# A hybrid diffusion trunk on one core: the two layers' tails put into a written order, the last parts' squares added by TensorE

## The chip, the cores and the metric

The kernel runs as one program on one core of a Trainium2 chip. A core has five engines with instruction streams of their own: TensorE (PE, with its weight loads PEld), VectorE (DVE), ScalarE (ACT), GpSimd (POOL) and SyncE (SP), which here issues the DMA transfers. [...] The metric is device time in microseconds, the median over the executions of a kernel.

## The reference

Two layers run over 1024 latent tokens and 256 context tokens, each of 1024 channels, in float32. What matters here stands at the end of a layer and at the start of the next:

```python
def rmsnorm(t, g):
    y = tf * lax.rsqrt(jnp.mean(tf * tf, axis=-1, keepdims=True) + EPS) * g
def modulate(t, shift, scale):
    return t * (1 + scale) + shift
for l in range(DEPTH):
    ax = modulate(rmsnorm(h, norm1_g[l]), mx[0], mx[1])      # and ac from hc, the context
    yx, yc = mixing_layer(ax @ w_in[l], ac @ w_in[l], ...)
    h = h + mx[2] * (yx @ w_out[l])
    h = h + mx[5] * conv_ffn(modulate(rmsnorm(h, norm2_g[l]), mx[3], mx[4]), w_up[l], ..., w_down[l])
    # the context hc likewise, in layer 0 alone
return rmsnorm(h, final_g)
```

So behind the last product with w_down, layer 0 normalises and modulates h and hc for layer 1, and layer 1 normalises h for the output. A token's mean of squares runs over all its 1024 channels, so no row of a token can be normalised before the last product for that token.

## The kernel before

Activations lie with channels on the 128 partitions and tokens along the free axis: h is eight tiles (k or o = 0 to 7) of 128 x 1024, the context hc eight of 128 x 256. Tokens are worked off in parts: part 0 and 1 are 512 latent tokens each, part 2 the 256 context tokens, and parts 3 and 4 are the two halves of part 1 (256 tokens each). A product in float32 is made of three passes over split operands (high times high, low times high, high times low; L1332 to L1334 in the tail).

The down projection has 22 blocks of 128 hidden channels. Twenty of them run in a loop of five chunks, the main loop (products at L939, each result added to h by VectorE in acc_h, L1244). That stretch stands inside `manual_schedule()`: what is written there keeps the written order on each engine, and a planner with a cost model places all other instructions between. The region is opened by `order.enter_context(tc.manual_schedule())` (L814) and closed by `order.close()` (L1310), right behind the loop.

Behind L1310 comes the tail, placed by the planner. Four operands (two blocks, two parts) are loaded and split by `pair` (copy to a high half L831 on ScalarE, low half L832 on VectorE). The last two blocks are multiplied by `down1(w, part, o)`, once for each part and each output tile o: six matmuls, then acc_h, then `sums[part].add` (L217): ScalarE squares the row (L219, L223), and VectorE or GpSimd adds it to an accumulator (L224). In layer 0 the parts are 0, 1, 2, in layer 1 they are 0, 3, 4.

`stats` (L226) sums the accumulator over partitions with TensorE (tile nps, L230), scales it on VectorE (L232) and takes the power -1/2 on GpSimd (L233). `spread` (L235) turns that into a row on all partitions: VectorE scales the identity by it (dg, L241), TensorE multiplies by ones (npb, L242).

In layer 0, `pipelined` writes: products of a part, its stats, the normalisation of the part before, its spread. The normalisation is `modulated` (L245): for each k one VectorE instruction (nt, L253), then ScalarE makes the high half and VectorE the low half (L260, L261); for k = 1, 4, 7 ScalarE adds the shift (L256) and casts (L257), and GpSimd makes the low half (L258). Rows of parts 0 and 1 are also stored to `h_dram` (L1368).

In layer 1 all three parts' products and sums come first; the scales of parts 0 and 3 are copied to SBUF by ScalarE (L1388), and `final` multiplies each row by gain and scale on VectorE (L1373) and stores it (L1374), part by part.

Scratch tiles (squares, normalised rows, scaled identities, accumulators, copies of scales) share one tag, "nt", with five buffers. PSUM has two banks for tag "g", two for "a", and two double ones for "bc".

Behind layer 0's tail layer 1 starts with products of the first two tiles of w_in (`feed`, L194 to L196), which fill the two "g" banks; ScalarE copies them out (L269, L299). Weights are brought in by `prefetch`, with `load_weights` (copy L179, L180 or L185, low half L181, L182 or L186).

## Time and profile before

| what | value |
|---|---|
| median of three runs | 3044.99 us (3044.64 to 3050.8) |
| profiled execution, its own time | 3046.27 us |
| span of its instructions | 3044.5 us |
| busy: TensorE / VectorE / ScalarE / GpSimd | 92% / 70% / 41% / 45% |
| mean granted TensorE clock | 0.956 |
| layer 0's tail: first product of the last two blocks | 1662.3 us |
| layer 1's tail: last product | 3012.5 us |

The profile gives the instructions of one execution with start, duration, source line and tiles, and infers from semaphores what ended an engine's idle time. Times count from the first instruction. A row of the timeline reads: start, duration, engine, line, operation, output tile <- input tiles, shapes, count, and in brackets idle time before it and what ended it. Neighbouring equal instructions are merged into one row with a count. A row by line gives minimum, median and maximum duration in ns. SPq stands for SyncE's issues of DMA transfers.

### The profile page before, as it was taken

To read this page: it belongs to the slowest core of one execution; us is meant where nothing else is said; L and a number is where in the kernel's file an instruction comes from. 1 tells how busy PE (TensorE), PEld (TensorE's weight loads), DVE (VectorE), ACT (ScalarE), POOL (GpSimd) and SP (SyncE) were. 2 spreads that over 40 slices of the span, in tenths; PEclk is the share of its full clock that TensorE was granted. 3 is DMA by queue.
4 is the path that set the end of the run, shared out by engine and by line. 5 is a ranking of instruction groups with operands and counts; after the bars stand their busy time and mean duration, and the time that the engine had idled before them with its cause. 6 is when DMAs were issued, how large, how long until landed. Compare 5 with 4: busy or idle time off the path is not lost. (4 is left out here: it accounts for less than half of the span.)

```text
span 3044.5 us, 40171 instructions
## 1 busy us (share of the span) xinstructions
PE 2786.5 (92%) x14430; PEld 2335.4 (77%) x14430; DVE 2141.4 (70%) x3484; ACT 1247.2 (41%) x2404; POOL 1357.0 (45%) x894
## 2 busy tenths in 40 slices
PE   6789989989989999998999799989988899998996
PEld 4678877878768888887888688877777688886775
DVE  7887745562777777788877654546557777877996
ACT  4345542232444344444333455542223444444332
POOL 4334343323334455544555244444243455554553
PEclk8899998989999999999999899999899999999998
DMA  6343322032133434346334112131251233336441
GB/s 219 89 113 113 96 87 77 31 141 70 56 104 127 144 127 144 130 142 204 117 125 123 51 46 67 46 103 59 77 180 56 90 118 121 118 114 205 135 145 63
DMA packets 167738, 332.54 MB, mean 109 GB/s; under 512 B 49650, under 2 KB 62834, under 8 KB 167282
## 3 DMA queue, kind: packets, MB, share of 16 engines
q1 hardware_dynamic: 167252, 328.81, 32.9%
q8 instruction: 114, 1.87, 0.2%
q10 hardware_dynamic: 288, 1.18, 0.1%
q14 instruction: 84, 0.69, 0.1%
HBM read 255.72 MB, written 74.19 MB: 108 GB/s over the span
## 5 line engine op out<-in xcount | busy, mean ns | idle before, releaser
L939 PE MATMUL ua<-ph,wu 128*128 128x512 f32 x1408 | 449.9, 401 | 31.4 <-DVE ub L1039 13.4
L165 POOL TENSOR_TENSOR wu<-urb,wu 128x512 fp32r<-128x512 f32 x160 | 244.4, 1528 | 323.8 <-ACT wu L164 323.8
L194 PE MATMUL gps<-xh,wh 128*128 128x512 f32 (+1 forms) x968 | 361.2, 374 | 15.6 <-ACT vt L269 7.0
L165 POOL TENSOR_TENSOR wu<-ura,wu 128x512 fp32r<-128x512 f32 x192 | 305.6, 1593 | 155.2 <-ACT wu L164 155.2
L195 PE MATMUL gps<-xh,wl 128*128 128x512 f32 (+1 forms) x968 | 356.1, 368 | 0.5 <-DVE wl L181 0.5
L196 PE MATMUL gps<-xl,wh 128*128 128x512 f32 (+1 forms) x968 | 355.9, 368 | 0.0
L939 PE MATMUL ubc<-ph,wu 128*128 128x512 f32 x1056 | 332.6, 396 | 15.1 <-DVE ubc L1036 6.5
L939 PEld LDWEIGHTS ua<-ph,wu 128*128 128x128 f32 x1408 | 263.9, 192 | 94.5 <-ACT ut L1033 17.3
L426 POOL TENSOR_SCALAR P<-P,rs 128x640 f32<-128x640 f32 (+2 forms) x108 | 215.6, 2008 | 237.2 <-DVE rs L421 130.3
L165 POOL TENSOR_TENSOR wu<-S,wu 128x512 fp32r<-128x512 f32 x128 | 180.7, 1414 | 248.3 <-ACT wu L164 247.0
L939 PE MATMUL ua<-pl,wu 128*128 128x512 f32 x704 | 280.1, 398 | 0.1
L164 ACT CAST wu<-S 128x512 fp32r<-128x512 f32 x128 | 79.4, 621 | 413.0 <-DVE S L162 404.8
L939 PEld LDWEIGHTS ubc<-ph,wu 128*128 128x128 f32 x1056 | 198.9, 191 | 60.9 <-issue 7.9
L186 POOL TENSOR_TENSOR wl<-wraw,wh 128x1024 fp32r<-128x1024 f32 x54 | 134.4, 2491 | 212.6 <-ACT wh L185 200.1
L194 PEld LDWEIGHTS gps<-xh,wh 128*128 128x128 f32 x968 | 186.9, 193 | 45.3 <-ACT vt L269 7.3
L939 PE MATMUL da<-ph,wu 128*128 128x512 f32 x640 | 202.8, 398 | 12.1 <-ACT wu L164 11.4
L939 PE MATMUL ubc<-pl,wu 128*128 128x512 f32 x528 | 208.3, 395 | 0.0
L195 PEld LDWEIGHTS gps<-xh,wl 128*128 128x128 f32 x968 | 186.6, 193 | 26.6 <-issue 1.0
L196 PEld LDWEIGHTS gps<-xl,wh 128*128 128x128 f32 x968 | 186.2, 192 | 26.1 <-issue 0.5
L164 ACT CAST wu<-ura 128x512 fp32r<-128x512 f32 x192 | 118.9, 622 | 129.3 <-DVE ura L162 72.8
L164 ACT CAST wu<-urb 128x512 fp32r<-128x512 f32 x160 | 99.4, 622 | 168.5 <-DVE urb L162 141.4
L939 PE MATMUL dbc<-ph,wu 128*128 128x512 f32 x480 | 150.7, 395 | 10.8 <-DVE c L1099 10.8
(296 smaller groups left out, 6858.9 us busy)
## 6 DMA issues: line engine op xcount, KB each, us to landing
gs<-g_dram SPq DMA_DIRECT2D x148, 256.0 KB, 2.8
wm<-in_w_mod_dram SPq DMA_DIRECT2D x56, 512.0 KB, 3.6
wmp<-in_w_mod_dram SPq DMA_DIRECT2D x112, 256.0 KB, 2.7
wraw<-in_w_in_dram SPq DMA_DIRECT2D x46, 512.0 KB, 3.6
ura<-in_w_up_dram SPq DMA_DIRECT2D x44, 512.0 KB, 4.2
urb<-in_w_up_dram SPq DMA_DIRECT2D x44, 512.0 KB, 5.2
g_dram<-gt SPq DMA_DIRECT2D x60, 256.0 KB, 3.1
g_dram<-c SPq DMA_DIRECT2D x44, 256.0 KB, 2.0
```

The costliest lines, as they stand in the source:

```text
L164: nc.scalar.copy(w[:, 0], b[name])
L165: nc.gpsimd.tensor_tensor(w[:, 1], b[name], w[:, 0].bitcast(F32), op=ALU.subtract)
L186: nc.gpsimd.tensor_tensor(wl.rearrange(flat), raw.rearrange(flat), wh.rearrange(flat).bitcast(F32), op=ALU.subtract)
L194: nc.tensor.matmul(ps[:, :n], wh[:, k], xh, start=k == 0, stop=False)
L195: nc.tensor.matmul(ps[:, :n], wl[:, k], xh, start=False, stop=False)
L196: nc.tensor.matmul(ps[:, :n], wh[:, k], xl, start=False, stop=k == KT - 1)
L426: nc.gpsimd.tensor_scalar(Pb[r][:, :w], Pb[r][:, :w], rs[:, r:r + 1], None, op0=ALU.mult)
L939: nc.tensor.matmul(ps, lt, rt, start=start and j == 0 and q == 0, stop=j == len(x) - 1 and q == 2, skip_group_check=True)
```

## The change

`order.close()` moves from behind the main loop to the end of the layer, so that the whole tail stands in written order. What is written there:

- `down1` only multiplies; `head(part, between)` runs it for the eight o and, behind each column's update and square, calls the functions listed for that o.
- Layer 0: products of part 0; products of part 1 with stats and spread of part 0 and its rows 0 to 3; products of part 2 with rows 4 to 6 of part 0 and the stats of part 1; row 7; the next weights (`prefetch`); spread and rows of part 1; stats, spread and rows of part 2. A row is one VectorE instruction, ScalarE's high half, and VectorE's low half (`settle`, one row behind) for every k; GpSimd makes no low halves here. The squares of part 0 are added by VectorE, those of parts 1 and 2 by GpSimd.
- Layer 1: products of part 0 (squares added by VectorE), of part 3 and of part 4. For parts 3 and 4 `add_pe` has no accumulator: TensorE sums each square over partitions straight into one PSUM tile, one column behind (`held`). Rows of part 0 go between the products of part 4; the others follow. For k = 1, 4, 7 of parts 0 and 3, ScalarE multiplies by the gain and GpSimd by the scale (from an SBUF copy made by `spread_copy`); all other rows are VectorE's, with the scale read from PSUM.

```diff
--- before.py
+++ after.py
@@ -213,6 +213,20 @@
             self.pool = pool
             self.part = part
             self.first = True
+            self.ps = None
+
+        def add_pe(self, h, psp, stop):
+            m = self.n // 128
+            if self.first:
+                self.ps = psp.tile([128, 4], F32, tag="bc" if psp is not psg else "g", name="nps")
+            sq = self.pool.tile([128, self.n], F32, tag="nt", name="sq", bufs=NT)
+            nc.scalar.activation(sq, h, AF.Square)
+            first, self.first = self.first, False
+
+            def held():
+                for j in range(m):
+                    nc.tensor.matmul(self.ps[:, j:j + 1], sq[:, j * 128:(j + 1) * 128], ones[:, 0:1], start=first and j == 0, stop=stop, skip_group_check=True)
+            return held
 
         def add(self, h, eng=None):
             if self.first:
@@ -225,8 +239,8 @@
 
         def stats(self, psp, ta):
             m = self.n // 128
-            ps = psp.tile([128, 4], F32, tag=ta, name="nps")
-            for j in range(m):
+            ps = self.ps or psp.tile([128, 4], F32, tag=ta, name="nps")
+            for j in range(m if self.ps is None else 0):
                 nc.tensor.matmul(ps[:, j:j + 1], self.acc[:, j * 128:(j + 1) * 128], ones[:, 0:1], start=True, stop=True)
             self.r = r = self.pool.tile([128, 4], F32, tag="rs", name="rs")
             nc.vector.tensor_scalar(r[:, :m], ps[:, :m], 1.0 / D, EPS, op0=ALU.mult, op1=ALU.add)
@@ -765,7 +779,7 @@
             return hs[0][k][:, o:o + n]
 
         def new_sums(parts):
-            return {part: Sums(part, npl, npl.tile([128, PARTS[part][1]], F32, tag="nt", name="acc", bufs=NT)) for part in parts}
+            return {part: Sums(part, npl, npl.tile([128, PARTS[part][1]], F32, tag="nt", name="acc", bufs=NT) if part < 3 else None) for part in parts}
 
         for k in range(KT):
             hsrc(k, h[k], None if last else hc[k])
@@ -1307,7 +1321,6 @@
                     ust.close()
                     wx = fp.enter_context(tc.tile_pool(name=f"wx{l}", bufs=1, side="right", reuse_waits="tile"))
         put_all()
-        order.close()
         xpool[0] = wx
         p = NF // 2 - 1
         gl_ = {}
@@ -1317,12 +1330,9 @@
             if not last:
                 gl_[i, 2] = gcs[NF - 2 + i]
 
-        def down1(w, part, o):
+        def down1(w, part, o, tag):
             o0, pn = PARTS[part]
-            if o % 2:
-                ps = psf.tile([128, 512], F32, tag="a", name="dps")
-            else:
-                ps = psg.tile([128, 512], F32, tag="g", name="dps")
+            ps = (psg if tag == "g" else psf).tile([128, 512], F32, tag=tag, name="dps")
             for i in range(2):
                 c0 = i * 512 + (o % 4) * 128
                 wh, wl = [t.rearrange("p a b -> p (a b)")[:, c0:c0 + 128] for t in w]
@@ -1332,8 +1342,7 @@
                 nc.tensor.matmul(ps[:, :pn], wh, gh, start=i == 0, stop=False)
                 nc.tensor.matmul(ps[:, :pn], wl, gh, start=False, stop=False)
                 nc.tensor.matmul(ps[:, :pn], wh, gl, start=False, stop=i == 1)
-            acc_h(o, part, ps)
-            sums[part].add(hv(o, part), nc.gpsimd if last and o % 2 else nc.vector)
+            return ps
 
         ws = [weights(), weights()]
         rawpool[0] = None
@@ -1345,50 +1354,93 @@
                 affine(1, 0, cd)
         Xn = [[None] * 3 for _ in range(KT)]
 
-        def pipelined(parts, head, tail):
-            prev = None
-            for part in parts:
-                head(part)
-                sums[part].stats(psf, "bc")
-                if prev is not None:
-                    tail(*prev)
-                prev = (part, sums[part].spread(psf, "bc"))
-            tail(*prev)
-
-        def down_head(part):
+        def head(part, between):
+            held = None
             for o in range(KT):
-                down1(ws[o // 4], part, o)
-
-        def down_tail(part, pb):
+                ps = down1(ws[o // 4], part, o, "a" if o % 2 or part == 4 else "g")
+                if held is not None:
+                    held()
+                acc_h(o, part, ps)
+                held = sums[part].add_pe(hv(o, part), psf if part == 3 else psg, o == KT - 1) if part > 2 else sums[part].add(hv(o, part), nc.vector if part == 0 else None)
+                for fn in between.get(o, ()):
+                    fn()
+            if held is not None:
+                held()
+
+        def modulate(part, ks):
+            n = PARTS[part][1]
+            cd = 1 if part == 2 else 0
+            A, B = aff[1][cd][:, 0:8], mod[1][cd][:, 0:8]
+
+            def go():
+                for k in ks:
+                    t = npl.tile([128, n], F32, tag="nt", name="nt", bufs=NT)
+                    nc.vector.scalar_tensor_tensor(t, hv(k, part), A[:, k:k + 1], pbs[part][:, :n], op0=ALU.mult, op1=ALU.mult)
+                    xh, xl = xtile(part)
+                    nc.scalar.activation(xh, t, AF.Identity, bias=B[:, k:k + 1])
+                    late.append((xl, t, B[:, k:k + 1], xh))
+                    if len(late) > 1:
+                        settle()
+                    Xn[k][part] = xh, xl
+                    if part < 2:
+                        o0 = PARTS[part][0]
+                        nc.sync.dma_start(h_dram[:, k, o0:o0 + n], hv(k, part))
+            return go
+
+        late = []
+
+        def settle():
+            xl, t, b, xh = late.pop(0)
+            nc.vector.scalar_tensor_tensor(xl, t, b, xh.bitcast(F32), op0=ALU.add, op1=ALU.subtract)
+
+        def final(part, ks):
             o0, n = PARTS[part]
-            res = modulated(1, 0, part, [hv(k, part) for k in range(KT)], pb, npl)
-            for k in range(KT):
-                Xn[k][part] = res[k]
-                if part < 2:
-                    nc.sync.dma_start(h_dram[:, k, o0:o0 + n], hv(k, part))
-
-        def final(part, pb):
-            o0, n = PARTS[part]
-            for k in range(KT):
-                nc.vector.scalar_tensor_tensor(hv(k, part), hv(k, part), fg[:, k:k + 1], pb[:, :n], op0=ALU.mult, op1=ALU.mult)
-                nc.sync.dma_start(out[k * 128:(k + 1) * 128, o0:o0 + n], hv(k, part))
-
+
+            def go():
+                for k in ks:
+                    v = hv(k, part)
+                    if part < 4 and k % 3 == 1:
+                        nc.scalar.mul(v, v, fg[:, k:k + 1])
+                        nc.gpsimd.tensor_tensor(v, v, copies[part], op=ALU.mult)
+                    else:
+                        nc.vector.scalar_tensor_tensor(v, v, fg[:, k:k + 1], pbs[part][:, :n], op0=ALU.mult, op1=ALU.mult)
+                    nc.sync.dma_start(out[k * 128:(k + 1) * 128, o0:o0 + n], v)
+            return go
+
+        copies = {}
+
+        def spread_copy(part, pool, tag):
+            spread(part, pool, tag)
+            n = PARTS[part][1]
+            copies[part] = npl.tile([128, n], F32, tag="nt", name="pbs", bufs=NT)
+            nc.scalar.copy(copies[part], pbs[part][:, :n])
+
+        st = lambda part: lambda: sums[part].stats(psf, "bc")
+        head(0, {})
         if last:
-            pbs = {p: npl.tile([128, PARTS[p][1]], F32, tag="nt", name="pbs", bufs=NT) for p in tail_parts[:-1]}
-            done = []
-            for part in tail_parts:
-                o0, n = PARTS[part]
-                down_head(part)
-                sums[part].stats(psf, "bc")
-                if part == tail_parts[-1]:
-                    for p in done:
-                        final(p, pbs[p])
-                    final(part, sums[part].spread(psf, "bc"))
-                else:
-                    nc.scalar.copy(pbs[part], sums[part].spread(psf, "bc")[:, :n])
-                    done.append(part)
+            head(3, {2: (st(0),), 6: (lambda: spread_copy(0, psf, "bc"),)})
+            head(4, {1: (st(3), final(0, (0, 1))), 4: (final(0, (2,)),), 5: (lambda: spread_copy(3, psg, "g"),), 6: (final(0, (3, 4)),)})
+            sums[4].stats(psf, "bc")
+            final(0, (5, 6, 7))()
+            final(3, (0, 1))()
+            spread(4, psf, "a")
+            final(3, range(2, KT))()
+            final(4, range(KT))()
         else:
-            pipelined(tail_parts, down_head, down_tail)
+            sp = lambda part: lambda: spread(part, psf, "bc")
+            head(1, {2: (st(0),), 4: (sp(0), modulate(0, (0,))), 5: (modulate(0, (1,)),), 6: (modulate(0, (2,)),), 7: (modulate(0, (3,)),)})
+            head(2, {2: (modulate(0, (4,)),), 3: (st(1),), 4: (modulate(0, (5,)),), 6: (modulate(0, (6,)),)})
+            modulate(0, (7,))()
+            settle()
+            prefetch()
+            sp(1)()
+            modulate(1, range(KT))()
+            settle()
+            st(2)()
+            sp(2)()
+            modulate(2, range(KT))()
+            settle()
+        order.close()
         fp.close()
         return Xn
 
```

## The prediction

> **What bounds the kernel now.** I read first the times of each engine by stretch (columns: stretch, its length, busy time and instructions of TensorE, its weight loads, VectorE, ScalarE, GpSimd, then granted clock, DMA share, GB/s). The kernel as a whole is TensorE's, 92% busy; the two ends of layers, which the change touches, are not:
>
> ```profile
> 1710.70:1726.80 16.10, 1.99 (x9) 1.45 (x8) 14.52 (x30) 12.49 (x24) 7.63 (x7) 0.65 0.00 1
> ...
> 2991.40:3012.80 21.40, 21.40 (x148) 19.71 (x146) 14.98 (x31) 5.46 (x11) 6.22 (x6) 1.00 0.00 1
> 3012.80:3044.50 31.70, 4.44 (x17) 3.71 (x16) 16.21 (x37) 5.30 (x15) 7.24 (x10) 0.55 0.36 132
> ```
>
> Behind the last product of layer 1 (3012.8) 31.7 us are left in which TensorE does 4.4 us. The chain of waits says what they are, and the list of waits agrees:
>
> ```profile
> 3014.64 3.39 DVE g L1373 x5
> ...
> 3018.89 0.73 POOL acc L224
> 3019.65 0.44 DVE acc L224
> ...
> 3035.43 0.74 POOLq L1657
> 3036.64 1.21 PE npb L242 x4
> ...
> 3038.74 2.35 DVE g L1373 x6
> ```
>
> ```profile
> PE nps L230 <- POOL acc L224: 17.6, 2, 9.5
> ```
>
> The reader is to see a serial chain: final rows of part 0, seven additions of squares of part 3 handed to and fro between GpSimd and VectorE, its scale, its rows, then all of it once more for part 4. TensorE waits 17.6 us for the two sums. Five "nt" buffers hold three sums and two copies of scales in this stretch, so a square gets a buffer late and the additions cannot run ahead.
>
> At the end of layer 0 it is VectorE and what follows it, by the timeline:
>
> ```profile
> 1725.46 0.72 POOL L258 TENSOR_TENSOR xl<-nt,xh 128x256 fp32r<-128x256 f32 x1 [0.92 <-ACT xh L257]
> ...
> 1726.22 0.59 ACT L269 COPY vt<-gps 128x512 f32<-128x512 f32 x1 [0.83 <-POOL xl L258]
> ...
> 1726.86 0.79 PE L194 MATMUL gps<-xh,wh 128*128 128x512 f32 x1 [7.03 <-ACT vt L269]
> ```
>
> Layer 1's products of part 0 already stand in both "g" banks; the copy that empties the first waits for the last normalised row (ends 1726.18). That end is what layer 1 starts from, so layer 0's gain is the shift of 1726.18.
>
> **The change part by part.**
>
> *Start of both tails.* The region of written order now runs on through the tail. The four operands of the last pair of column blocks (VectorE, L832) were pulled forward by the planner; written out, they stand behind the last update of the loop.
>
> ```profile
> 1662.28 0.40 PE L1332 MATMUL dps<-ph,wh 128*128 128x512 f32 x1
> 1662.48 0.48 DVE L1244 SCALAR_TENSOR_TENSOR hd<-dc,mod,hd 128x256 f32<-128x256 f32 x1
> ...
> 1663.44 0.39 PE L1334 MATMUL dps<-pl,wh 128*128 128x512 f32 x1
> 1663.65 2.40 POOL L186 TENSOR_TENSOR wl<-wraw,wh 128x1024 fp32r<-128x1024 f32 x1 [4.49 <-DMA cb<-in_rpbU_dram]
> ```
>
> ```profile
> L832 DVE TENSOR_TENSOR pl<-gs,ph x4: 681/688/694, 1640.7 to 1646.0; 128x512 fp32r<-128x512 f32 x4
> ```
>
> ```profile
> L832 DVE TENSOR_TENSOR pl<-gs,ph x4: 678/1060/1540, 2971.9 to 2979.0; 128x512 fp32r<-128x512 f32 x4
> ```
>
> The first column's last product needs the third of them: 1662.96 + 3 x 0.69 = 1665.0 in place of 1663.44, +1.6 us in layer 0. The next layer's weight subtraction (2.40 us on GpSimd) now falls onto them, and the second L832 row shows what that does: 1.54 us in place of 0.69. Bounds 0 and 2.4 us; I take 1.9, since the subtraction starts before the third.
>
> *Layer 0, parts 0 to 2.* Removed from VectorE: additions of parts 1 and 2 (to GpSimd). Added: all the low halves that GpSimd did for every third row. Moved: normalisation of part 0 into the products of parts 1 and 2. Rows that price it:
>
> ```profile
> 1674.92 0.75 DVE L1244 SCALAR_TENSOR_TENSOR g<-dps,mod,g 128x512 f32<-128x512 f32 x1
> ...
> 1676.32 0.75 DVE L1244 SCALAR_TENSOR_TENSOR g<-dps,mod,g 128x512 f32<-128x512 f32 x1
> ```
>
> ```profile
> 1682.87 1.01 POOL L233 TENSOR_TENSOR rs<-rs,nhalf 128x4 f32<-128x4 f32 x1 [16.82 <-DVE rs L232]
> ```
>
> ```profile
> 1683.91 0.87 DVE L241 TENSOR_SCALAR dg<-ident,rs 128x128 f32<-128x128 f32 x4 [1.12 <-POOL rs L233]
> ```
>
> ```profile
> 1697.48 2.71 DVE L253 SCALAR_TENSOR_TENSOR nt<-g,aff,npb 128x512 f32<-128x512 f32 x4
> ...
> 1715.57 1.41 DVE L261 SCALAR_TENSOR_TENSOR xl<-nt,mod,xh 128x512 fp32r<-128x512 f32 x2
> ...
> 1719.94 1.66 DVE L253 SCALAR_TENSOR_TENSOR nt<-hd,aff,npb 128x256 f32<-128x256 f32 x4
> ```
>
> A column of products takes 1.40 us; a row of 512 needs 0.66 + 0.67 = 1.33 us of VectorE (pitches of L253 and L261), a row of 256 about 0.79, an update 0.66 or 0.40. I count from part 1's first product, 1674.92 - 1.47 = 1673.45 before, 1675.05 with the 1.6. Part 0's scale is asked for at column 2, but its power stands on GpSimd behind the additions of columns 1 and 2 (1.30 us each), so it is ready at about 8; column 4's products end at 7.8, the four VectorE scalings (0.87) and TensorE's spreading end at 10.1, and TensorE waits for them. Then update, row, low half alternate with columns 5 to 7: VectorE is done at 17.4. Through part 2: eight updates 3.2, three rows 4.0, scale 0.1, last row and two low halves 2.0: 26.6. Behind it the next layer's weight half 0.7, spreading of part 1 1.5, eight rows 10.6 and the last low half 0.4: 39.8. Part 2's scale now stands alone in the written order (0.1, power 0.7, scalings 0.5, spreading 1.2, with hand-overs 2.7): 42.5. Eight rows of 256 at 0.79 and a last 0.4: 49.2. End 1724.2, 2.0 us earlier than 1726.18; with the 1.9 above, 0.1.
>
> What speaks against even this is the pairing of VectorE with GpSimd:
>
> ```profile
> 2996.97 1.30 POOL L224 TENSOR_TENSOR acc<-acc,sq 128x512 f32<-128x512 f32 x1 [8.45 <-ACT sq L223]
> ```
>
> ```profile
> L261 DVE SCALAR_TENSOR_TENSOR xl<-nt,mod,xh x15: 472/742/1774, 1695.8 to 1724.7; 128x512 fp32r<-128x512 f32 x10, 128x256 fp32r<-128x256 f32 x5
> ```
>
> The low halves, 0.74 us as a rule, took up to 1.77. In the new order each part 1 or part 2 column sends a square to GpSimd's addition just when VectorE reaches a low half. Seven low halves lie there, three against 1.30 us additions and four against the 0.7 us ones: at worst 3 x 1.1 + 4 x 0.6 = 5.7, at best nothing. By times of arrival they are within 0.1 us of each other, so I take half, 2.8. Layer 0: -2.0 + 1.9 + 2.8 = **+2.7 us**, between -2.0 and +6.1.
> [...]
>
> *Layer 1.* Fourteen products of this tail stood inside the loop, in front of the loop's last products:
>
> ```profile
> L1332 PE MATMUL dps<-ph,wh x6: 389/392/397, 2976.0 to 2988.7; 128*128 128x512 f32 x6
> ...
> L1333 PE MATMUL dps<-ph,wl x4: 392/394/397, 2976.3 to 2982.5; 128*128 128x512 f32 x4
> ...
> L1334 PE MATMUL dps<-pl,wh x4: 390/392/396, 2977.0 to 2982.7; 128*128 128x512 f32 x4
> ```
>
> ```profile
> 2991.39 0.39 PE L939 MATMUL da<-pl,wu 128*128 128x512 f32 x1
> ```
>
> ```profile
> 3005.36 0.48 DVE L1244 SCALAR_TENSOR_TENSOR g<-dps,mod,g 128x256 f32<-128x256 f32 x1 [0.22 <-PE dps L1334]
> 3006.07 0.48 DVE L1244 SCALAR_TENSOR_TENSOR g<-dps,mod,g 128x256 f32<-128x256 f32 x1 [0.23 <-PE dps L1334]
> ```
>
> ```profile
> 3007.30 0.95 PE L230 MATMUL nps<-ones,acc 128*128 128x1 f32 x8
> 3008.12 0.36 PE L1332 MATMUL dps<-ph,wh 128*128 128x256 f32 x1
> ...
> 3010.34 1.06 PE L242 MATMUL npb<-dg,ones 128*128 128x128 f32 x8
> ```
>
> ```profile
> 3018.06 0.42 ACT L223 ACTIVATE sq<-g 128x256 f32<-128x256 f32 x1 [4.11 <-DVE g L1373]
> ```
>
> At 1.40 / 6 = 0.23 us each they are 3.2 us. TensorE was fully busy there, so I let the loop end 3.2 earlier (bound: not at all, if they filled stalls): free at 2988.4. Part 0: 8 x 1.38 = 11.0, plus 1.85 for the operands: 3001.25. Part 3: eight columns of 0.71 us, eight sums of squares (four of the eight L230 instructions, 0.45, and 0.05 of change-over: 0.5), sum and spreading of part 0 (0.9 each: eight L230 in 0.82, eight L242 likewise, and change-over), and a last square with nothing in front (0.6): 5.7 + 4.0 + 2.4 = 12.1, to 3013.3. Part 4: 5.7 + 4.0 + spreading 0.5 + 0.6 = 10.8, to 3024.1. A square is ready 1.1 us after its column (update 0.48, square 0.42, hand-overs); the next column and the sum ahead of it cover 0.71 + 0.5 = 1.21, so it costs nothing as long as ScalarE and VectorE are free; if that 0.1 us is gone, each microsecond of lateness counts sixteen times.
>
> Removed: the adding chains behind 3012.8. What remains behind 3024.1 are 19 output rows, bounded by SP's issues:
>
> ```profile
> 3038.37 0.81 SPq L1374 DMA_DIRECT2D out_dram<-g  x2
> ```
>
> ```profile
> 3041.78 0.41 SPq L1374 DMA_DIRECT2D out_dram<-g  x1
> ```
>
> The last eight issues took 3.41 / 7 = 0.49 us apiece while VectorE made a row each 0.39 (2.35 / 6), so SP sets the pace; the span ended 2.3 us behind the last. From the last sum: first issue at +1.0, the third row waits for GpSimd behind its power (+2.4), the rest at 0.49: last issue ends at +10.9, end +13.2, at 3037.3. Layer 1: **-7.2 us**, between -4.0 (the 3.2 us were stalls) and -9.8 (VectorE's rows alone set the end: 10.6 behind the last sum).
>
> *Sum.* +2.7 - 7.2 = -4.5. The profiled execution took 3046.27 us (span 3044.5 and 1.8 around it), so 3041.8 for one like it; it lies 1.3 above the median of 3044.99, so I forecast **3040.5 us**. Its own range is 3036 to 3045.
>
> **The rivals.**
> *Faster.* Additions and low halves miss each other, the weight subtraction comes late enough, and output rows leave as fast as VectorE makes them: -2.0 - 9.8 = -11.8, 3033.2 us. For it: updates read PSUM and never showed a stretched time (0.75 in every row). Against: the L261 row, and 0.49 us for SP.
> *The sums do not shorten the tail.* ScalarE has row products and copies of its own among the squares; if these put each square 0.5 us past its cover, 16 x 0.5 = 8.0 eats the gain of layer 1: 2.7 + 0.8 = +3.5, 3048.5 us. Against it: ScalarE was busy 5.46 of 21.4 us in these products.
> *Slower.* The planner may no longer bring layer 1's first products into the longer written region. Then their 48 (11.0 us at 0.23) come behind the end of layer 0's tail in place of inside it: -4.5 + 11.0 = +6.5, 3051.5 us. It decides once more than about 20 of the 48 (4.5 us) start behind that end. Against it: the fourteen products above came from outside the old region and ran inside it.
>
> **How the numbers follow.** Forecast 0.48, faster 0.30, sums too late 0.10, slower 0.12. A measurement of this kernel can tell about 0.2%, 6.1 us, from no change: faster means under 3038.9, slower over 3051.1. Under 3038.9 lie nearly all of the faster case and a quarter of the forecast's own range: 0.41. Over 3051.1 lies about two thirds of the slower case and a little of the one before: 0.09. The rest, 0.50, is the same. The range 3032 to 3049.5 takes in the faster and the late-sum case and leaves most of the slower one out.
>
> **What would show it.** The L832 operands of both tails behind the last loop update, with TensorE idle about 2 us. Layer 0: the last low half at about 1729, L261 rows over 1.2 us while GpSimd adds. Layer 1: the 16 pairs of sums between columns of 0.71, TensorE busy until about 3024, last issue 0.49 us behind the one before. I am wrong if layer 0's end comes before 1724, if SP is not the last to finish, or if layer 1's first products start only behind the tail.

## The result

The changed kernel takes 3071.22 us (median of 4 executions, 3063.3 to 3075.48), the kernel before 3044.85 (3044.64 to 3050.8) beside it: a ratio of 1.0068, 95% interval 1.0052 to 1.0084 (the ratios here and below are those on record; they are not quotients of the two medians, which here would give 1.0087). It is slower, by more than a measurement of this kernel can confuse with no change, and it lies outside the forecast range (3032 to 3049.5, with 3040.5 forecast).

The profiled execution took 3063.3 us (span 3061.5), the shortest of the four and the one with the highest mean granted clock (0.955; the others 0.950 to 0.954). Since executions lie some 12 us apart, the traces are compared by stretches inside one execution, from one TensorE instruction to another that both kernels have: **A** runs from the 455th product of the group dc to the 1676th of the group gps (layer 0's tail and the first products of the mixing), **B** from the 856th product of the group da to the end of the span (end of the last loop and layer 1's tail). A grew from 120.2 to 129.0 us, B from 99.6 to 113.9. What lies between them took 1173.8 and 1172.2. So both tails lost, 8.8 and 14.3 us, where +2.7 and -7.2 had been forecast.

### The profile page after: what moved, and what is told of

The parts are those of the page before. It is cut to its first block, busy times and chain, and to the rows that moved or that the text cites. A ratio compares the mean times of both kernels' runs of the same rounds, so it can differ in the third digit from the quotient of the medians.

```text
span 3061.5 us, 40260 instructions
## 1 busy us (share of the span) xinstructions
PE 2805.3 (92%) x14486; PEld 2350.8 (77%) x14486; DVE 2134.2 (70%) x3471; ACT 1248.7 (41%) x2401; POOL 1359.0 (44%) x893
## 5 line engine op out<-in xcount | busy, mean ns | idle before, releaser
L953 PE MATMUL ubc<-ph,wu 128*128 128x512 f32 x1056 | 333.2, 397 | 14.7 <-ACT wu L164 6.3
L164 ACT CAST wu<-S 128x512 fp32r<-128x512 f32 x128 | 79.5, 621 | 418.6 <-DVE S L162 394.5
```

The source lines that it names most:

```text
L164: nc.scalar.copy(w[:, 0], b[name])
L953: nc.tensor.matmul(ps, lt, rt, start=start and j == 0 and q == 0, stop=j == len(x) - 1 and q == 2, skip_group_check=True)
```

## The profile after

In layer 1, stretch by stretch (columns: stretch, length, busy time and instructions of TensorE, its weight loads, VectorE, ScalarE, GpSimd, granted clock, DMA share, GB/s):

```profile
2991.00:3003.90 12.90, 11.69 (x51) 8.89 (x50) 9.18 (x14) 3.16 (x5) 0.00 (x0) 1.00 0.00 0
3003.90:3011.40 7.50, 1.85 (x13) 1.44 (x11) 5.07 (x9) 2.35 (x5) 0.00 (x0) 0.83 0.00 0
...
3012.20:3046.30 34.10, 33.31 (x155) 33.05 (x155) 9.65 (x24) 7.12 (x17) 2.97 (x3) 0.50 0.06 24
3046.30:3049.70 3.40, 1.56 (x13) 1.39 (x12) 1.60 (x5) 2.70 (x6) 2.07 (x3) 0.99 0.40 154
```

Before, TensorE was done at 3012.8 and waited for chains of additions. Now it issues almost without a pause for 34.1 us (33.31 busy), at half its clock. Two things come ahead of that: part 0's products are over at 3003.9, and then TensorE does 1.85 us of work in 7.5. VectorE's timeline shows why:

```profile
2995.82 0.75 DVE L1258 SCALAR_TENSOR_TENSOR g<-dps,mod,g 128x512 f32<-128x512 f32 x1 [0.65 <-PE dps L1344]
2997.27 0.69 DVE L238 TENSOR_TENSOR acc<-acc,sq 128x512 f32<-128x512 f32 x1 [0.70 <-ACT sq L237]
2997.88 0.75 DVE L1258 SCALAR_TENSOR_TENSOR g<-dps,mod,g 128x512 f32<-128x512 f32 x1
2999.33 0.69 DVE L238 TENSOR_TENSOR acc<-acc,sq 128x512 f32<-128x512 f32 x1 [0.70 <-ACT sq L237]
2999.93 0.75 DVE L1258 SCALAR_TENSOR_TENSOR g<-dps,mod,g 128x512 f32<-128x512 f32 x1
...
3009.76 0.69 DVE L238 TENSOR_TENSOR acc<-acc,sq 128x512 f32<-128x512 f32 x1 [0.76 <-ACT sq L237]
```

Update, wait 0.70 us for ScalarE's square of the row just updated, addition, next update: a column takes 2.05 us of VectorE (2997.88 to 2999.93) where its products take 1.40. The next update could have run in the wait, but the written order puts it behind the addition. Eight columns later TensorE stands and waits for the square of part 3's first column, whose update came last in that line:

```profile
3011.41 1.01 PE L228 MATMUL nps<-ones,sq 128*128 128x1 f32 x4 [5.59 <-ACT sq L223]
...
3017.55 0.85 PE L228 MATMUL nps<-ones,sq 128*128 128x1 f32 x4
3019.68 0.85 PE L228 MATMUL nps<-ones,sq 128*128 128x1 f32 x4
```

Behind the stall of 5.59 us, a column of part 3 (six products of 256 columns and four one-column matmuls) takes 2.13 us (3017.55 to 3019.68), at the clock of 0.50.

Layer 0 has the same VectorE line, with GpSimd's weight subtractions falling on it:

```profile
1661.02 0.74 DVE L1258 SCALAR_TENSOR_TENSOR g<-dps,mod,g 128x512 f32<-128x512 f32 x1
...
1663.79 2.62 DVE L238 TENSOR_TENSOR acc<-acc,sq 128x512 f32<-128x512 f32 x1 [0.70 <-ACT sq L237]
...
1667.78 0.69 DVE L238 TENSOR_TENSOR acc<-acc,sq 128x512 f32<-128x512 f32 x1 [0.70 <-ACT sq L237]
...
1669.83 1.99 DVE L238 TENSOR_TENSOR acc<-acc,sq 128x512 f32<-128x512 f32 x1 [0.70 <-ACT sq L237]
...
1680.12 2.06 DVE L1258 SCALAR_TENSOR_TENSOR g<-dps,mod,g 128x512 f32<-128x512 f32 x3
...
1732.13 0.49 DVE L1394 SCALAR_TENSOR_TENSOR xl<-nt,mod,xh 128x256 fp32r<-128x256 f32 x1 [0.18 <-ACT xh L1380]
```

```profile
1663.48 2.39 POOL L186 TENSOR_TENSOR wl<-wraw,wh 128x1024 fp32r<-128x1024 f32 x1
...
1668.87 2.40 POOL L186 TENSOR_TENSOR wl<-wraw,wh 128x1024 fp32r<-128x1024 f32 x1
```

This execution ran 4.4 us ahead of before's when it came to the tail; the last low half's end, 1732.6, is 1737.0 by before's time, against 1726.18.

## The experiments

The table gives A and B of each profiled execution and the median of all executions of that kernel. The changed kernel was measured beside four executions of the kernel before (median 3044.85), the other kernels on three chips beside 10 to 31 further ones, which ran from 3044 to 3060 us (medians 3050.5 to 3052.1). So a difference from the kernel before is taken from the executions beside it, and A and B tell more than a few us of the median. They scatter too: A is 118.8 to 120.2 in the seven kernels with the planner's layer 0, and 129.0, 129.0 and 132.0 in the three with the changed kernel's (the last with 27.3 us of A at half clock, the other two with 17.1).

| kernel | A | B | median, us | ratio to before, 95% |
|---|---|---|---|---|
| before | 120.2 | 99.6 | 3044.85 | |
| changed | 129.0 | 113.9 | 3071.22 | 1.0068 (1.0052 to 1.0084) |
| additions one column late | 125.2 | 97.2 | 3063.31 | 1.0043 (1.0026 to 1.0060) |
| the stall filled with matmuls | 129.0 | 101.4 | 3062.9 | 1.0040 (1.0023 to 1.0056) |
| written order in layer 0 only | 132.0 | 101.3 | 3063.96 | 1.0049 (1.0034 to 1.0065) |
| written order in layer 1 only | 119.7 | 115.8 | 3064.17 | 1.0038 (1.0021 to 1.0056) |
| layer 1 only, additions late | 119.5 | 109.3 | 3049.13 | 1.0000 (0.9987 to 1.0013) |
| the same, no sums on TensorE | 120.2 | 93.5 | 3044.08 | 0.9975 (0.9964 to 0.9987) |
| both layers, late, operands early | 123.3 | 109.5 | 3060.93 | 1.0034 (1.0017 to 1.0050) |
| layer 1 only, late in turn, operands early | 120.1 | 106.0 | 3054.57 | 1.0014 (1.0001 to 1.0026) |
| the same, no sums on TensorE | 120.2 | 92.8 | 3042.8 | 0.9972 (0.9960 to 0.9985) |
| sums kept, products repeated | 118.8 | 100.0 | 3050.49 | 1.0003 (0.9990 to 1.0016) |
| both layers, a weight split put off | 125.8 | 103.9 | 3059.13 | 1.0028 (1.0012 to 1.0043) |
| both layers mended | 125.0 | 93.5 | 3048.57 | 0.9992 (0.9982 to 1.0002) |

### First theory: the VectorE line stalls TensorE, and the stall costs the clock

**Additions one column late.** In part 0 of both layers, a column's square is added behind the next column's update:

```
+ if held is not None: held()      # the addition of the column before
+ held = sums[0].add_late(hv(o, 0), nc.vector)   # square now, addition later
```

> Edit: in both layers VectorE adds part 0's square one column late, behind the update of the next column; nothing else. Theory A (VectorE's line update-square-add makes a column 2.05 us instead of 1.40; TensorE then stands still 5.6 us before the first sum of squares; behind that standstill its clock stays at half through parts 3 and 4): part 0's columns go to about 1.4 us, the standstill in layer 1 falls under 1 us, the clock stays at 1.0 until the last sum, a column of parts 3 and 4 takes 1.2 us in place of 2.13. Layer 0's tail about 5 us shorter, layer 1's about 5 + 15 = 20 us: some 25 us under the changed kernel, near 3040. Rival B (the one-column sums of squares throttle TensorE by themselves, standstill or not): the columns of parts 3 and 4 still take 2.13 us, only 5 us per layer are won, about 10 us under the changed kernel.

**The stall filled.** The changed kernel, with 24 matmuls that compute nothing of use put into layer 1's stall (extra work):

```
+ if part == 3 and o == 1:
+     busy(24)
```

> Edit: 24 unused matmuls of 128x512 (about 0.23 us each, 5.5 us) stand on TensorE in layer 1 behind part 3's second column, where it stood still for 5.6 us; all else as in the changed kernel. Theory A (the standstill brings the clock down, and the light columns cannot bring it back): the clock stays at 1.0, columns of parts 3 and 4 take 1.2 us, 16 x 0.9 = 14 us under the changed kernel although there is more work. Rival B (the sums throttle by themselves): no change within 2 us.

In both executions profiled the half clock is gone from layer 1's tail. The windows of the kernel with late additions (first its stall, now 1.78 us), and two of its columns:

```profile
3017.50:3020.20 2.70, 0.92 (x9) 0.71 (x7) 2.35 (x5) 1.12 (x3) 0.00 (x0) 1.00 0.00 0
3020.20:3030.40 10.20, 9.86 (x80) 9.44 (x80) 3.69 (x11) 2.99 (x7) 1.01 (x1) 1.00 0.01 2
```

```profile
3024.75 0.61 PE L228 MATMUL nps<-ones,sq 128*128 128x1 f32 x4
...
3026.01 0.50 PE L228 MATMUL nps<-ones,sq 128*128 128x1 f32 x4
```

The same columns now take 1.25 to 1.26 us (3024.75 to 3026.01) at a clock of 1.00, and B is 97.2, under before's. With the stall filled B is 101.4, 12.5 less than in the changed kernel for more work:

```profile
3024.50:3034.60 10.10, 9.76 (x80) 9.25 (x79) 3.40 (x12) 3.21 (x8) 1.01 (x1) 1.00 0.01 2
```

So the tail can run at the full clock, and one-column matmuls do not bring it down by themselves (1.00 was granted from 3020.2 to 3043.6 with late additions, from 3024.5 to 3048.1 with the stall filled). But the medians came down by 8 us only, or by 15 if each is taken over the kernel before beside it (26.4, then 11.2 and 10.8), and not by the 25 that had been expected of the first kernel. The next two kernels say where the rest is.

**One layer at a time.** The written order in one layer, the planner's order of the kernel before in the other:

> Edit: the written order in layer 0's tail alone; layer 1's tail as in the kernel before. By the two traces layer 0's tail lost 9.8 us, so 9 to 11 us over the kernel before, near 3054. If the planner gives it back further on, under 5 us.

> Edit: the written order in layer 1's tail alone; layer 0's tail as in the kernel before. By the two traces layer 1's tail lost 14 us (17 behind the loop, less 3 for the fourteen products that no longer stand in the loop): near 3059, with the clock at half from the first sum of squares on. If the half clock is a matter of the longer way before it, it does not come and the time is near 3042.

The losses add: A is long where layer 0 is written (132.0), B where layer 1 is (115.8), and each kernel is 12 us over the one before beside it (3052.11) by the median. Layer 1 alone has executions at 3054.8 and 3054.85 and four others at 3061.8 to 3068.6: the gap is about what the half clock costs. So an execution seems to fall into the half clock or not. Only one execution of each kernel has records of its stretches, but the mean granted clock over the span is on record for every one: 0.955 and 0.956 in the two short ones, 0.950 to 0.952 in the four others. Thirty us at half clock make 0.005 of it, so the fall fits, though the mean does not say where it lies. By the same number the late additions did less than their trace says: 0.957 in the execution profiled, the shortest, and 0.951 to 0.955 in the other three. With the stall filled all five have 0.956 to 0.959.

### Second theory: sparse columns, and chance

The next four kernels were to find the best version of layer 1, and three of them upset the theory.

**Layer 1 only, additions late.**

> Layer 0 as in the kernel before; layer 1 in the written order, with the addition of a square in part 0 put one column later. Stretch A is from the 455th product of the group dc to the 1676th product of the group gps on TensorE (layer 0's tail and the start of the mixing; 120.2 us before, 129.0 in the changed kernel), stretch B from the 856th product of the group da to the end (layer 1's tail; 99.6 before, 113.9 changed, 97.2 where both layers had the late addition). If the two tails are independent: A about 120, B about 97, and the time 2 to 3 us under the kernel before. If the late addition's gain in layer 1 was the luck of one execution: B scatters between 97 and 114 from one execution to another, and the median lies 3 to 10 us above the kernel before.

**The same without sums on TensorE.** The squares of parts 3 and 4 go back into accumulators, in turn on VectorE and GpSimd, still in the written order:

```
- held = sums[part].add_pe(hv(o, part), ...)
+ held = sums[part].add_late(hv(o, part), nc.gpsimd if part > 2 and o % 2 else nc.vector)
```

> As the run with layer 1 alone and the late addition, but the squares of the last two parts are added into accumulators again, in turn by VectorE and GpSimd, one column late, instead of by one-column matmuls. My theory (the sums on TensorE are harmless at the full clock: 1.25 us a column against 0.71 without them, covered by VectorE and ScalarE): columns of the last parts 0.75 to 1.2 us, set by VectorE and GpSimd; stretch B 94 to 99, within 3 us of the run with the sums on TensorE. Rival (the sums cost what they add to TensorE, 16 times 0.5 us): B about 8 us shorter, near 89. Third: GpSimd's slower addition sets the pace or the lighter TensorE loses its clock, B over 100.

**Operands early, both layers.** The last four operands (L846) are read and split between the loop's last updates; sums on TensorE kept:

```
+ if early and ch == NCH - 1 and half == 1 and i >= len(names) - 4 and i < len(names) - 2:
+     lead(i - len(names) + 4)     # load, then ScalarE's half; VectorE's half follows an update
```

> The changed kernel with the late addition in part 0 of both layers, and with the four operands of the last chunk read and split two to four weight groups earlier, between the loop's last updates, in both layers. If the operands behind the last update lie on the path as forecast (2.49 us on VectorE): stretch B 96 (97.2 with the late addition alone, minus 1.0 to 1.2, since TensorE's first column of 1.4 us then takes their place), stretch A 123 to 124 (125.2 alone). If VectorE's total work is the bound of layer 0's tail, A falls by the whole 2.5 us to 122.7. If something else is late there (TensorE waits for the spread rows): A stays at 125.

**Layer 1 only, operands early, part 0's additions late and in turn on VectorE and GpSimd.**

> Layer 0 as in the kernel before; layer 1 in the written order with the late addition, the additions of part 0 in turn on VectorE and GpSimd, and the operands split early. VectorE then has 1.09 us of work per column of 1.40, so that TensorE doesn't wait at the first sum (1.78 us with all additions on VectorE): stretch B 97.2 - 1.1 - 1.8 = 94.3, the time about 5 us under the kernel before. If GpSimd's 1.29 us and VectorE's slowing beside it eat that: B 96 to 97. If the stall only moves (to the spread of part 0 or to SP's output rows, which take 13 us behind the last product either way): the part of the stall comes back and B is 96.

Early operands gave layer 0 what was expected (A 123.3 for 125.2). In layer 1 the three kernels with sums fell to half clock in the executions profiled. With late additions B had been 97.2; the same layer 1 now gave 109.3, at half clock from 3010.4, with the same stall of 1.78 us:

```profile
3010.40:3045.00 34.60, 33.44 (x157) 33.08 (x155) 10.14 (x25) 8.31 (x19) 4.24 (x4) 0.50 0.08 31
```

That execution (3060.49 us) is the second longest of twelve, whose median is 3049.13 and whose mean clocks go from 0.950 to 0.959, so most of them did better. And the last kernel, whose stall is only 0.93 us, fell too:

```profile
2998.90:3010.20 11.30, 11.29 (x54) 9.37 (x54) 8.29 (x13) 4.90 (x8) 3.88 (x3) 1.00 0.00 0
...
3010.90:3014.40 3.50, 3.20 (x27) 3.21 (x28) 0.77 (x3) 1.05 (x3) 1.08 (x2) 0.99 0.00 0
3014.40:3045.00 30.60, 29.79 (x139) 29.43 (x137) 9.49 (x23) 7.31 (x17) 3.79 (x4) 0.50 0.09 35
```

TensorE is busy 3.20 of the 3.50 us ahead of the fall. The stall alone is not the cause, and busy time does not protect the clock. Without the sums, B is 93.5 and the kernel is 0.25% faster than before. "Harmless at the full clock", as I had expected of the sums, holds only in part: B is 3.7 under the 97.2 with them, where at most 3 was expected and 8 would have been the rival's. And the full clock is not to be had reliably with them.

What the clock follows was then worked out from the matmul records of all traces. The granted clock changes only at steps of 3.41 us. In a dense stretch of the kernel before, 55 products of 512 columns touch a window of 12.00 us, 2347 columns a us:

```profile
2984.00:2996.00 12.00, 12.00 (x55) 9.85 (x54) 6.64 (x10) 0.00 (x0) 2.41 (x1) 1.00 0.01 1
```

Two of the 55 began ahead of the window, so the dense rate itself is 4% lower (2261), and dense steps come out at 0.96; 2347 serves as the unit alone. The table has the columns of the products that began in each step of 3.41 us as a share of it, in the 14 traces:

| share streamed | steps at full clock, of them followed by full | steps at half clock, of them followed by full |
|---|---|---|
| under 0.2 | 309, 2 | 312, 2 |
| 0.2 to 0.3 | 106, 37 | 171, 8 |
| 0.3 to 0.4 | 363, 265 | 212, 55 |
| 0.4 to 0.45 | 237, 225 | 81, 78 |
| 0.45 to 0.55 | 311, 311 | 328, 328 |
| over 0.55 | 9916, 9916 | 1, 1 |

Over 0.45 the full clock was never lost (10227 steps); under 0.2 nearly always (307 of 309). A column with sums streams 6 x 256 = 1536 columns. In 1.25 us that is 1229 a us, a share of 0.52: kept, with little to spare. A stall, or the eight one-column matmuls of part 0's sum, in the same step bring it into the range where it may fall (the last step ahead of the fall at 3014.4 streamed 0.35). In 2.13 us at half clock it is 721 a us, 0.31, where most steps stay at half (157 of 212). So once fallen, this tail mostly stays down, but not always: in the kernel with a weight split put off, whose layer 1 is the one with late additions and early operands, it fell at 3012.5 and was back at the full clock from 3033.0, still among thin columns, with B 103.9 where the other execution had 109.5. (Some matmul records are missing: of the four one-column matmuls at 3004.80 in the kernel with products repeated, three stand. And how products across the border of a step are counted moves single counts by a tenth and more; both blur the bounds.)

Where the borders of the steps fall goes with what looked like chance. The stall of 1.78 us stands in four of the traces. Where the clock held (B 97.2), the step around the stall began 1.6 us ahead of it, took in all twelve products of part 3's first two columns and streamed 0.38; in the three that fell it began 0.2 to 1.1 us ahead and streamed 0.19, 0.26 and 0.26. Four traces suggest this and do not prove it.

Busy time alone does not bring the clock back either: from 3012.2 to 3046.3 in the changed kernel TensorE was busy 33.31 of 34.10 us, and the granted clock stayed at 0.50.

**Products repeated.** The kernel just described, with sums, and the first product of each column of parts 3 and 4 issued four more times (extra work, overwritten by the fifth):

```
+ for again in range(4 if i == 0 and part > 2 else 0):
+     nc.tensor.matmul(ps[:, :pn], wh, gh, start=True, stop=False, skip_group_check=True)
```

> The kernel with layer 1 alone, alternating additions and early operands, with sums on TensorE, whose clock fell to half at 3014.4 and whose stretch B was 106.0; and in each column of the last two parts the first product is issued four more times (extra work: 4 x 256 columns more, 0.43 us at the full clock, 16 times 6.8 us). Theory (the clock follows how many columns TensorE streams: a column with sums streams 1536 in 1.25 us, 0.51 of the full rate, and falls under about 0.4 with a small stall; at half clock it streams 1536 in 2.13 us, 0.30, and cannot get back): with the extra products 2560 in 1.68 us, 0.63; the clock stays at 1.0 to the end of part 4 in the profiled execution, stretch B 94.3 + 6.8 = 101, five us less than with less work, and the executions lie closer together than 3043.7 to 3063.1. Rival (the one-column matmuls bring the clock down by themselves, whatever else streams): half clock again, B 106 + 13.6 = 120. Rival (the fall is decided before, by the stall at the first sum): half clock in some executions still, spread as before.

The full rate in it is twice that of the products at half clock in the kernel that fell at 3014.4 (4 x 256 columns from 3015.90 to 3016.75, 1205 a us); of the unit above the shares are 0.52, 0.31 and 0.65.

```profile
3006.41 0.50 PE L228 MATMUL nps<-ones,sq 128*128 128x1 f32 x4
...
3008.05 0.50 PE L228 MATMUL nps<-ones,sq 128*128 128x1 f32 x4
```

```profile
3012.20:3031.20 19.00, 15.75 (x131) 15.36 (x130) 8.13 (x18) 7.49 (x17) 4.29 (x5) 1.00 0.18 70
```

A column takes 1.64 us and streams 2560 columns, a share of 0.67; the clock is 1.00 to the end of part 4, and B is 100.0 where 101 was expected. More work, 6.0 us less than without it (106.0). The two executions profiled lie at opposite ends of their twelves, but the mean clocks of all bear it out: 0.955 to 0.961 with the products repeated, 0.950 to 0.959 without; 0.953 to 0.960 in the three kernels without sums. The median is 4.1 us lower too, which the intervals alone would not show, since they overlap. The repeated products also closed the stall of 0.93 us ahead of the first sum, so this kernel does not part the stall from the thin columns; the one with the stall filled, whose columns stayed thin (steps of 0.39 to 0.58), kept its clock too. The executions still lie 15 us apart (3044.4 to 3059.7), about as far as those of the kernel before on this chip, so that part of the scatter is not this tail's.

### What is left of layer 0, and the best version

**No sums, part 4's squares on VectorE alone** (layer 1 only, operands early):

> Layer 0 as in the kernel before. Layer 1 in the written order, operands split early, part 0's additions one column late in turn on VectorE and GpSimd; no sums on TensorE: part 3's squares are added in turn by VectorE and GpSimd, part 4's by VectorE alone, so that GpSimd's multiplications of finished rows no longer stand ahead of an addition (they kept the last sum back until 3019.6 where GpSimd added in part 4 too, 4.7 us behind the last column). Theory (the written order pays once the one-column matmuls are gone): stretch B 93.5 - 1.1 (operands) - 2 to 4 (last sum) = 88 to 91, the time 7 to 11 us under the kernel before, and executions as close to each other as before's. Rival (SP's output rows bound the end whatever comes before): B stays at 93.

```profile
L1269 DVE SCALAR_TENSOR_TENSOR g<-dps,mod,g 128x256 f32<-128x256 f32 x16 | 7.6, 479 | 3.9 <-PE dps L1380 3.9
L238 DVE TENSOR_TENSOR acc<-acc,sq 128x256 f32<-128x256 f32 x10 | 6.0, 598 | 0.1
```

It has the lowest median, 0.9972 of before and 7.8 us under it, as much as expected; from the first kernel without sums (0.9975) the intervals do not tell it. But B is 92.8, hardly under 93.5: the rival had its number. The last sum came 78.9 us into B (79.5 in the first kernel without sums), because final rows on VectorE and stretched additions (598 ns on the mean: one of 1.27 us, two of 1.91 together, the other seven of 0.41 or 0.42; that GpSimd stretched them is my estimate from layer 0) took what the order gave, and the 13 us of rows behind it remained.

**A weight split put off.** Both layers written, late additions, operands early; in layer 0 one of GpSimd's subtractions moved behind part 2:

> The changed kernel with late additions and early operands in both layers (stretch A 123.3), and in layer 0 the next layer's first weights are split only where part 1's rows begin, so that one of the three 2.4 us subtractions on GpSimd no longer falls into part 0's additions (two additions took 2.01 and 2.30 us there instead of 0.68). If these collisions are what is left of layer 0's loss: stretch A 121.5 to 122. If TensorE's waits for the spread rows (3.05 and 0.69 us at the first spread, 1.4 at part 1's sum, 1.2 at part 2's spread) set it: A 123 as before. If the subtraction put off now falls among part 0's rows or delays the mixing's first products: A 124 to 126.

```profile
1709.93 0.79 PE L194 MATMUL gps<-xh,wh 128*128 128x512 f32 x1 [6.68 <-ACT wh L185]
```

All seven additions of part 0 took 0.68 or 0.69 us, so the collisions were gone, but A was 125.8, not under 123.3: the third outcome. The mixing's first product now waits 6.68 us for its weights. With A scattering by 3 us between executions of one layer 0, the rise itself is not shown; that nothing was gained is.

**Both layers mended.** As the kernel with the lowest median, with layer 0 written too, and there part 0's spread and rows one column later:

> Both layers in the written order. Layer 1 as in the kernel that beat the one before (operands early, late additions, no sums on TensorE; stretch B 92.8). Layer 0 with operands early and late additions (stretch A 123.3), and there part 0's spread and its eight rows one column of part 1 later, where the spread's scale is ready. If TensorE's wait for that spread (3.05 and 0.69 us) is what is left of layer 0's loss: A 120 to 121, and the time equals that of the kernel with layer 1 alone, about 7.5 us under before. If VectorE's total work in its written order is the bound (the rows only start later): A 123 to 125, the time 3 to 5 us above the kernel with layer 1 alone, 3 to 5 us under before.

A is 125.0: starting the rows later gains nothing that can be seen, and the time is 1.9 us under the kernel before beside it, where 3 to 5 were the least expected. Layer 0's written order costs 3 to 5 us of A even with both mends, and the planner's order is the better one there. Which of its rows set that was not settled.

## Why the prediction was wrong

**Layer 1 before its sums.** That the fourteen hoisted products free 3.2 us was right: the loop's last product starts 3.3 earlier (2990.84 - 2.8 against 2991.39). The four operands behind the last update came as forecast, 2.49 us on VectorE, with TensorE waiting 0.98 + 0.23 for them where 1.85 had been priced. The step that failed is "Part 0: 8 x 1.38 = 11.0": right for TensorE, but the part is over when VectorE is. I priced its update and its addition and not the square between them (0.70 us of waiting for ScalarE), which the written order puts in line: 2.05 us a column. The first sum came 5.9 us later than forecast (3011.41 - 2.8 = 3008.6 by before's time, against 3002.7).

**The sums.** The term "eight columns of 0.71, eight sums 0.5" was right at the full clock, 1.25 us measured for 1.21. The prediction nowhere asked which clock these columns would be granted. That is the second step that failed, a term left out: at 0.50 they took 2.13, and 16 x 0.92 = 14.7 us. With the 5.9 and about 1 us of small waits that is the 21.5 us between -7.2 and +14.3. In the execution with late additions at full clock the rest can be counted too: first sum 2.9 us late (a stall of 1.78 and about 1 before it), columns 16 x 0.04 and waits of 0.74, 0.32 and 0.48 together 2.1; and -7.2 + 5.0 = -2.2, measured -2.4.

**Behind the last sum** 13.2 us were forecast, with SP's issues as the bound; 12.95 were measured (from 3048.55), and SP was the last to issue.

**Layer 0.** The step that failed is its first: counting from part 1's first product, at 1675.05. VectorE reached part 1's first update at 1680.12, 1684.5 by before's time, against 1676.5: 8.0 us late, seven times 0.65 for the squares and 3.2 for the two stretched additions. Of this I had priced 1.9, and for another pair: the weight subtraction was to stretch the operands, but these took 2.49 us for all four. Behind that update 50.5 us were forecast (47.7 and 2.8 for low halves that collide) and 52.5 passed, so the last low half came 8.1 us late (1737.0 against 1728.9). The terms in there were not as forecast. Low halves hardly collided,

```profile
L1394 DVE SCALAR_TENSOR_TENSOR xl<-nt,mod,xh 128x512 fp32r<-128x512 f32 x16 | 12.4, 773 | 0.4
```

16 x 31 ns over the usual 742, 0.5 us for the forecast 2.8. The four scalings of the identity for part 0's spread did, beside two of GpSimd's additions (1.26 us each, from 1685.91 and 1687.37),

```profile
1686.48 2.43 DVE L255 TENSOR_SCALAR dg<-ident,rs 128x128 f32<-128x128 f32 x4
```

2.43 us for the 0.87 that I took from the trace of before, and TensorE waited 1.54 and 0.75 us for them. They are as long in the kernels with layer 0 mended (2.5 to 2.7 us), and no run took that away, so they may be part of the 3 to 5 us left there. The mixing gave 2 us back, which leaves A at +8.8. VectorE and GpSimd did collide in this tail, but not where the prediction had priced it: two of part 0's additions took 2.62 and 1.99 us for 0.69, each ending 0.54 or 0.55 us behind a subtraction of GpSimd (2.39 us from 1663.48, 2.40 from 1668.87).

**The rivals.** "The sums do not shorten the tail" had the right place and the right factor of sixteen, with another mechanism and half the price. The slower rival did not happen: layer 1's first products still ran inside the region. None of the three signs I had named for being wrong came up, and yet the time was 30 us off: the list guarded the parts I had thought about, not the two I had left out, a latency inside a written line and the granted clock. The account above is of the execution profiled, 17.0 us over before's; the median of the four lies 8 us higher still. The lower mean clocks of the other three point at more time at half clock, but where is not on record.

## What to carry to other kernels

When an order is written out by hand, price each engine's line with the latencies of the hand-overs inside it, not with its busy times (here 0.70 us of waiting made a column 2.05 us of VectorE where its products took 1.40); an instruction that needs another engine's answer belongs one step behind that engine's next input. When work moves to TensorE as one-column matmuls, ask what share of columns it still streams: here a tail at 0.52 of the unit above kept its clock only when nothing else went wrong, and at half clock, at 0.31, it came back in one of the traces that fell ahead of its last columns, and in the others stayed down nearly to the end. An experiment that adds work and gets faster (B 100.0 for 106.0 here) is a quick way to see such a clock.

## What the hardware showed that I had not expected

TensorE ran 34.1 us at half clock while 33.31 of them were busy, and a kernel with 4 x 256 more columns per column of products kept the full clock (1.00) through the same parts. Over 0.45 of the unit above, none of 10227 steps of 3.41 us at full clock was followed by half clock; under 0.4 at half clock, 65 of 695 steps were followed by full. Programs with the same layer 1 tail and the same stall fell in one profiled execution (B 109.3) and not in another (97.2), with the borders of the steps lying otherwise against the stall, so one trace does not settle a question about the clock; the mean granted clocks of all executions go further.
